# Column sums of a 32768 x 2048 matrix: float16 casting loads and pairwise adds against float32 loads folded in one vector instruction

## The chip, the cores and the metric

The kernel runs on one core of a Trainium2 chip. The core has a tensor engine (PE, matmuls, with PEld for its weight loads), a vector engine (DVE), a scalar engine (ACT), GpSimd (POOL) and a sync engine (SP). SP, ACT and POOL can issue DMA transfers between HBM and the on-chip memory SBUF; the transfers run on 16 DMA engines. Matmul results go to the accumulator memory PSUM. The metric is device time in microseconds. Lower is better.

## The reference

```python
def setup_inputs():
    batch, seq, dim = 32, 1024, 2048
    return {"grad_output": np.random.randn(batch, seq, dim).astype(np.float32)}

def reference(grad_output):
    return np.sum(grad_output, axis=(0, 1)).astype(np.float32)
```

The input is 32768 rows of 2048 float32 numbers, 268.44 MB. The output is one row of 2048 sums.

## The kernel before, in words

The input is seen as a matrix of 32768 rows. A load of m "rows" takes m x 128 matrix rows and gives each of the 128 SBUF partitions m whole matrix rows that lie one behind the other in HBM (`"(p m) d -> p (m d)"`). One row of such a load is 128 x 2048 float32, 1 MiB. The whole input is 256 of them.

A plan, made in Python before anything is issued, lists the loads in order: two float32 loads of one row, issued by SP (PRE_TILES, PRE_ENGS); 30 loads of 8 rows (BULK_M); one of 2; a taper of 4 and 2 (BULK_TAPER); five of one row (TAIL_TILES); and the last row in four column pieces of 512 (COL_SPLIT_LAST). All but the first two are issued by POOL and cast from float32 to float16 on the way (line 146). The 8-row tiles rotate through three buffers (T_BUFS).

For each load of two or more rows DVE adds the first half of the tile to the second half in float16 (line 152), which leaves half as many rows in a tile `c`. PE then multiplies each 512-column piece of `c` by a column of ones (line 161), which sums over the 128 partitions, and accumulates into one of four PSUM banks, one for each quarter of the 2048 columns. One-row tiles go to PE directly. At the end ACT and DVE copy the four banks to SBUF, two each (lines 175 and 177), and SP writes the 8 KB result (line 178).

The order on each engine is that of the program text; a framework inserts the waits. A load into a used buffer waits for the DVE add that read it; an add waits for its load; the matmuls wait for the add.

Of the kernel before, what the change touches and what calls it, by code (L numbers as in the profile page):

```python
# [1 line left out]

# [4 lines left out]

P = 128
MM_N = 512  # L10

PRE_TILES = 2
PRE_M = 1
PRE_ENGS = ("sync", "sync")
BULK_M = 8
BULK_TAPER = (4, 2)
USE_DVE = True
TAIL_TILES = 5
COL_SPLIT_LAST = True
T_BUFS = 3  # L20
C_BUFS = 3
TAIL_BUFS = 8
BULK_ENGS = ("gpsimd",)
OUT_COPY_ENGS = ("scalar", "vector")


@with_exitstack
def kernel(
    ctx: ExitStack,
    tc: tile.TileContext,  # L30
    grad_output: bass.AP,
    out: bass.AP,
):
    nc = tc.nc
    fp32 = mybir.dt.float32
    fp16 = mybir.dt.float16

    D = out.shape[-1]
    flat = grad_output.rearrange("b s d -> (b s) d")
    R = flat.shape[0]  # L40
    assert R % P == 0 and D % MM_N == 0
    nbanks = D // MM_N
    n_row_blocks = R // P

    pre_tiles = min(PRE_TILES, n_row_blocks // PRE_M // 4)
    col_split = COL_SPLIT_LAST and nbanks > 1
    taper = [m for m in BULK_TAPER if m < BULK_M]
    n_small = TAIL_TILES + (1 if col_split else 0)
    while pre_tiles * PRE_M + sum(taper) + n_small > n_row_blocks:
        if TAIL_TILES and n_small > 1:  # L50
            n_small -= 1
        elif taper:
            taper = taper[1:]
        else:
            col_split = False
            n_small = min(n_small, 1)
            break
    n_tail = n_small - (1 if col_split else 0)

    plan: list = []  # L60
    row = 0
    for i in range(pre_tiles):
        plan.append((row, PRE_M, fp32, PRE_ENGS[i % len(PRE_ENGS)], 0, D))
        row += P * PRE_M
    tail_start = R - P * (n_small + sum(taper))
    bi = 0
    while row < tail_start:
        take = min(P * BULK_M, tail_start - row)
        plan.append((row, take // P, fp16, BULK_ENGS[bi % len(BULK_ENGS)], 0, D))
        bi += 1  # L70
        row += take
    for m in taper:
        plan.append((row, m, fp16, BULK_ENGS[bi % len(BULK_ENGS)], 0, D))
        bi += 1
        row += P * m
    for _ in range(n_tail):
        plan.append((row, 1, fp16, BULK_ENGS[bi % len(BULK_ENGS)], 0, D))
        bi += 1
        row += P
    if col_split:  # L80
        for b in range(nbanks - 1, -1, -1):
            plan.append((row, 1, fp16, BULK_ENGS[bi % len(BULK_ENGS)], b * MM_N, MM_N))
            bi += 1
        row += P
    assert row == R

    io_pool = ctx.enter_context(tc.tile_pool(name="io", bufs=T_BUFS))
    pre_pool = None
    if pre_tiles:
        pre_pool = ctx.enter_context(tc.tile_pool(name="pre", bufs=pre_tiles))  # L90
    c_pool = None
    if USE_DVE:
        c_pool = ctx.enter_context(tc.tile_pool(name="csum", bufs=C_BUFS))
    n_small_tiles = n_tail + (nbanks if col_split else 0)
    tail_pool = None
    if n_small_tiles:
        tail_pool = ctx.enter_context(
            tc.tile_pool(name="tail", bufs=min(n_small_tiles, TAIL_BUFS))
        )
    const_pool = ctx.enter_context(tc.tile_pool(name="const", bufs=1))  # L100
    psum_pool = ctx.enter_context(tc.tile_pool(name="psum", bufs=1, space=bass.MemoryType.PSUM))

    ones16 = const_pool.tile([P, 1], fp16)
    nc.vector.memset(ones16[:], 1.0)  # L104
    ones32 = None
    if pre_tiles:
        ones32 = const_pool.tile([P, 1], fp32)
        nc.vector.memset(ones32[:], 1.0)  # L108

    accs = [  # L110
        psum_pool.tile([1, MM_N], fp32, tag=f"psum{b}", name=f"psum{b}")
        for b in range(nbanks)
    ]
    res = const_pool.tile([1, D], fp32)

    def uses_dve(entry) -> bool:
        _, m, dt_, _, _, col_n = entry
        return USE_DVE and dt_ is fp16 and m > 1 and col_n == D

    def n_chunks(entry) -> int:  # L120
        _, m, dt_, _, _, col_n = entry
        n = (m * col_n) // MM_N
        return n // 2 if uses_dve(entry) else n

    total_mm = [0] * nbanks
    for e in plan:
        for j in range(n_chunks(e)):
            total_mm[((e[4] + j * MM_N) % D) // MM_N] += 1
    started = [False] * nbanks
    n_mm = [0] * nbanks  # L130

    for i, entry in enumerate(plan):
        row0, m, dt_, eng_name, col_lo, col_n = entry
        rows = flat[row0 : row0 + m * P]
        if col_n == D:
            src = rows.rearrange("(p m) d -> p (m d)", p=P)
        else:
            src = rows[:, col_lo : col_lo + col_n]

        if dt_ is fp16:  # L140
            big = m > 1 and col_n == D
            pool, tag = (io_pool, "T") if big else (tail_pool, "Ttail")
            T = pool.tile([P, m * col_n], fp16, tag=tag, name=f"t{i}")
        else:
            T = pre_pool.tile([P, m * col_n], fp32, tag="Tpre", name=f"t{i}")
        getattr(nc, eng_name).dma_start(out=T[:], in_=src)  # L146

        red = T
        if uses_dve(entry):
            half = (m * col_n) // 2  # L150
            C = c_pool.tile([P, half], fp16, tag="C", name=f"c{i}")
            nc.vector.tensor_tensor(  # L152
                out=C[:], in0=T[:, :half], in1=T[:, half:], op=mybir.AluOpType.add
            )
            red = C

        w = ones16 if dt_ is fp16 else ones32
        for j in range(n_chunks(entry)):
            b = ((col_lo + j * MM_N) % D) // MM_N
            n_mm[b] += 1  # L160
            nc.tensor.matmul(  # L161
                accs[b][:, :],
                lhsT=w[:],
                rhs=red[:, j * MM_N : (j + 1) * MM_N],
                start=(not started[b]),
                stop=(n_mm[b] == total_mm[b]),
            )
            started[b] = True

    bank_order = list(range(nbanks - 1, -1, -1)) if col_split else list(range(nbanks))  # L170
    for k, b in enumerate(bank_order):
        eng = OUT_COPY_ENGS[k % len(OUT_COPY_ENGS)]
        dst = res[:, b * MM_N : (b + 1) * MM_N]
        if eng == "scalar":
            nc.scalar.copy(out=dst, in_=accs[b][:, :])  # L175
        else:
            nc.vector.tensor_copy(out=dst, in_=accs[b][:, :])  # L177
    nc.sync.dma_start(out=out[None, :], in_=res[:])


# [1 line left out]
_INS = ['grad_output']  # L182
_OUTS = [((2048,), 'float32')]


# [23 lines left out]
```

## Time and profile before

| | |
|---|---|
| timed runs | 628.96 us median of 3 (628.45 to 629.14) |
| profiled execution | span 627.2 us from the first to the last instruction; the profile holds no other time of this execution |
| PE | busy 195.1 us (31%), 536 matmuls, mean granted clock 0.65 of full |
| DVE | busy 138.9 us (22%), 37 instructions |
| POOL | busy 22.6 us (4%), 42 of its instructions issue loads |
| DMA | queue of the casting loads: 6048 packets, 133.17 MB written, 98.9% of the 16 engines' span |
| HBM | 268.44 MB read, 428 GB/s over the span |

A row of instructions names the line in the kernel, the engine, the operation, what it writes and reads (out<-in) with sizes, how often, the busy time and the mean duration in ns, and then the idle time of the engine ahead of it with what ended that idle time. The page's DMA row gives the busy share of the DMA engines in 40 equal slices of the span, as one digit each in tenths (9 is 90% or more). Bytes in the DMA queues are those written, so a casting load counts half of what it reads.

### The profile page before, as it was taken

To read this page: it belongs to the slowest core of one execution; us is meant where nothing else is said; L and a number is where in the kernel's file an instruction comes from. 1 tells how busy PE (TensorE), PEld (TensorE's weight loads), DVE (VectorE), ACT (ScalarE), POOL (GpSimd) and SP (SyncE) were. 2 spreads that over 40 slices of the span, in tenths; PEclk is the share of its full clock that TensorE was granted. 3 is DMA by queue.
4 is the path that set the end of the run, shared out by engine and by line. 5 is a ranking of instruction groups with operands and counts; after the bars stand their busy time and mean duration, and the time that the engine had idled before them with its cause. 6 is when DMAs were issued, how large, how long until landed. Compare 5 with 4: busy or idle time off the path is not lost.

```text
span 627.2 us, 1267 instructions
## 1 busy us (share of the span) xinstructions
PE 195.1 (31%) x536; PEld 58.1 (9%) x536; DVE 138.9 (22%) x37; ACT 2.4 (0%) x3; POOL 22.6 (4%) x46
## 2 busy tenths in 40 slices
PE   3323320333203333123341134321333312343165
PEld 0001100011000111001110011100111000111011
DVE  0202222022220122211222202222022221122320
ACT  0000000000000000000000000000000000000000
POOL 1000000000000000000000000000000000000110
PEclk9677556775567665667655776656676567665677
DMA  9999999999999999999999999999999999999997
GB/s 242 226 234 201 234 201 234 202 232 203 232 203 232 203 232 203 232 204 230 205 230 205 230 205 230 205 230 206 228 207 228 207 224 211 224 211 221 206 206 139
DMA packets 6344, 135.36 MB, mean 216 GB/s; under 512 B 705, under 2 KB 1217, under 8 KB 1857
## 3 DMA queue, kind: packets, MB, share of 16 engines
q0 software_dynamic: 6048, 133.17, 98.9%
q1 hardware_dynamic: 290, 2.11, 0.9%
q8 instruction: 4, 0.07, 0.0%
q14 instruction: 2, 0.02, 0.0%
HBM read 268.44 MB, written 0.01 MB: 428 GB/s over the span
## 4 chain that ended last, share of the span: by engine, by line
another core or an unknown queue 66%; DVE 21%; DMA 11%; PE 1%; POOL 1%; issue 0%; DVEq 0%; POOLq 0%
DVE c L152 20%; DMA t<-in_grad_output_dram 11%; PE psum L161 1%; POOL t L146 1%; DVEq L152 0%; DVE res L177 0%; POOLq L193 0%
## 5 line engine op out<-in xcount | busy, mean ns | idle before, releaser
L161 PE MATMUL psum<-c,ones 128*1 128x512 f16 x496 | 175.9, 533 | 405.5 <-DVE c L152 405.5
L152 DVE TENSOR_TENSOR c<-t 128x8192 f16<-128x8192 f16 (+2 forms) x33 | 137.5, 4167 | 471.1 <-DMA t<-in_grad_output_dram 471.1
L161 PEld LDWEIGHTS <-ones 128*1 128x1 f16 x520 | 56.5, 109 | 537.5 <-issue 516.4
L146 POOL DMA_DIRECT2D t<-in_grad_output_dram x42 | 22.4, 538 | 590.4 <-DVE c L152 575.3
L161 PE MATMUL psum<-t,ones 128*1 128x512 f16 (+1 forms) x40 | 19.4, 639 | 23.5 <-DMA t<-in_grad_output_dram 23.5
L177 DVE COPY res<-psum 1x512 f32<-1x512 f32 x2 | 1.4, 679 | 13.9 <-PE psum L161 13.9
L161 PEld LDWEIGHTS psum<-t,ones 128*1 128x1 f32 x16 | 1.6, 106 | 27.5 <-DMA t<-in_grad_output_dram 14.1
L175 ACT COPY res<-psum 1x512 f32<-1x512 f32 x2 | 1.1, 575 | 621.1 <-PE psum L161 621.1
L175 ACT ACT_TABLE_LOAD x1 | 1.3, 1283 | 0.7 <-PEq L193 0.7
L104 DVE MEMSET ones<- 128x1 f16 x1 | 0.1, 59 | 0.8 <-PEq L193 0.8
L193 POOL MEMSET const-float32-0.0<- 128x1 f32 x1 | 0.1, 100 | 0.2 <-issue 0.2
L193 POOL MEMSET const-bfloat16-1.0<- 128x1 bf16 x1 | 0.1, 103 | 0.0
L193 POOL MEMSET const-float32-1.0<- 128x1 f32 x1 | 0.1, 100 | 0.0
L193 POOL MEMSET const-uint8-127<- 128x1 uint8 x1 | 0.1, 100 | 0.0
L108 DVE MEMSET ones<- 128x1 f32 x1 | 0.1, 59 | 0.0
## 6 DMA issues: line engine op xcount, KB each, us to landing
t<-in_grad_output_dram POOLq DMA_DIRECT2D x30, 4096.0 KB, 53.1
t<-in_grad_output_dram POOLq DMA_DIRECT2D x5, 512.0 KB, 20.4
t<-in_grad_output_dram SPq DMA_DIRECT2D x2, 1024.0 KB, 14.3
t<-in_grad_output_dram POOLq DMA_DIRECT2D x2, 1024.0 KB, 26.6
t<-in_grad_output_dram POOLq DMA_DIRECT2D x1, 2048.0 KB, 29.0
t<-in_grad_output_dram POOLq DMA_DIRECT2D x4, 128.0 KB, 16.1
out_dram<-res SPq DMA_DIRECT2D x1, 8.0 KB
```

The source lines that it names most:

```text
L104: nc.vector.memset(ones16[:], 1.0)
L108: nc.vector.memset(ones32[:], 1.0)
L146: getattr(nc, eng_name).dma_start(out=T[:], in_=src)
L152: nc.vector.tensor_tensor(out=C[:], in0=T[:, :half], in1=T[:, half:], op=mybir.AluOpType.add)
L161: nc.tensor.matmul(accs[b][:, :], lhsT=w[:], rhs=red[:, j * MM_N : (j + 1) * MM_N], start=(not started[b]), stop=(n_mm[b] == total_mm[b]),)
L175: nc.scalar.copy(out=dst, in_=accs[b][:, :])
L177: nc.vector.tensor_copy(out=dst, in_=accs[b][:, :])
L193: nc = _bacc.Bacc("TRN2", target_bir_lowering=False, num_devices=1)
```

## The change

The kernel body is written anew. All loads are float32 and issued by SP. UNITS lists them: 7, 8 and 7 rows ten times over, then 7, 7, 6, 4, 3, 2, 2, 2, 2 (39 units, 255 rows); the last row comes in two pieces, three quarters of the columns and one quarter. The units rotate through three slots of one SBUF tile `ring`; a slot has room for its 7 or 8 rows and one more row in front. For i of 3 and up, SP waits until unit i-3 has been summed by PE (`s_free`) before it issues unit i.

For a unit of m > 2 rows, DVE folds the rows 1 to m-1 into the row in front with one `tensor_reduce`, whose view of the rows runs over m innermost, so that consecutive elements read lie 2048 elements apart. For a unit of 2 rows DVE only passes a semaphore on. PE then sums the folded row and the unit's row 0 (or the two rows of a 2-row unit) over the partitions: 8 float32 matmuls of 512 columns, in which quarter g of the columns goes to column group 32 x g of the array and to PSUM partition 32 x g. The three first quarters share one bank, the last has its own. These matmuls stand in a hardware loop of 13 rounds over the three slots. After the sums of slots 0 and 1, PE also runs six float16 matmuls of a zero tile into a spare bank (FILL).

At the end DVE copies the three first quarters and SP writes them; ACT copies the last quarter and writes it itself; POOL waits for both. The PSUM banks are set to zero by DVE at the start, as no matmul starts an accumulation. The code stands in a `tile_critical` block, in which the waits are written by hand; the program has an additional rendezvous of the engines with POOL where the block begins and one where it ends.

The core of the diff, with the planning code, the pools and the final launch code left out:

```diff
-BULK_M = 8
-BULK_TAPER = (4, 2)
-TAIL_TILES = 5
-BULK_ENGS = ("gpsimd",)
+SLOTS = (7, 8, 7)
+UNITS = SLOTS * 10 + (7, 7, 6, 4, 3, 2, 2, 2, 2)
+FILL = (6, 6, 0)
...
-            T = pool.tile([P, m * col_n], fp16, tag=tag, name=f"t{i}")
-        getattr(nc, eng_name).dma_start(out=T[:], in_=src)
-            nc.vector.tensor_tensor(
-                out=C[:], in0=T[:, :half], in1=T[:, half:], op=mybir.AluOpType.add
-            )
-        for j in range(n_chunks(entry)):
-            b = ((col_lo + j * MM_N) % D) // MM_N
-            nc.tensor.matmul(
-                accs[b][:, :],
-                lhsT=w[:],
-                rhs=red[:, j * MM_N : (j + 1) * MM_N],
...
+    def sums(at, c0=0, w=D):
+        for g in range(4):
+            lo, hi = max(c0, g * Q), min(c0 + w, (g + 1) * Q)
+            if lo < hi:
+                mm = t.matmul(
+                    (acc if g < 3 else accr)[32 * g : 32 * g + 1, lo - g * Q : hi - g * Q],
+                    lhsT=ones[:],
+                    rhs=ring[:, at + lo - c0 : at + hi - c0],
+                    start=False,
+                    stop=False,
+                    tile_position=(0, 32 * g),
+                    skip_group_check=True,
+                )
+        return mm
...
+        for i, m in enumerate(UNITS):
+            s = i % len(SLOTS)
+            at = base[s] + (D if m > 2 else 0)
+            src = flat[row * P : (row + m) * P].rearrange("(p m) d -> p (m d)", p=P)
+            if i >= len(SLOTS):
+                q.wait_ge(s_free, i - len(SLOTS) + 1)
+            q.dma_start(out=ring[:, at : at + m * D], in_=src).then_inc(landed[s], 16)
+            row += m
+        at = base[-1] + 2 * D
+        for c0, w, s in ((0, 3 * Q, last[0]), (3 * Q, Q, last[1])):
+            q.dma_start(
+                out=ring[:, at + c0 : at + c0 + w], in_=flat[row * P :, c0 : c0 + w]
+            ).then_inc(s, 16)
...
+        for i, m in enumerate(UNITS):
+            s = i % len(SLOTS)
+            r1 = base[s] + 2 * D
+            v.wait_ge(landed[s], 16 * (i // len(SLOTS) + 1))
+            if m > 2:
+                v.tensor_reduce(
+                    out=ring[:, base[s] : base[s] + D],
+                    in_=ring[:, r1 : r1 + (m - 1) * D].rearrange("p (m d) -> p d m", m=m - 1),
+                    op=add,
+                    axis=X,
+                ).then_inc(red[s], 1)
+            else:
+                v.sem_inc(red[s], 1)
+        t.wait_ge(s_one, 4)
+        with t.Fori(0, len(UNITS) // len(SLOTS)) as _:
+            for s in range(len(SLOTS)):
+                t.wait_ge(red[s], 1)
+                t.sem_inc(red[s], -1)
+                sums(base[s])
+                sums(base[s] + D).then_inc(s_free, 1)
+                for _ in range(FILL[s]):
+                    t.matmul(
+                        junk[0:1, :],
+                        lhsT=fill[:, :1],
+                        rhs=fill[:],
+                        start=True,
+                        stop=True,
+                        tile_position=(0, 0),
+                    )
+        t.wait_ge(last[0], 16)
+        sums(at, 0, 3 * Q).then_inc(s_end[0], 1)
+        t.wait_ge(last[1], 16)
+        sums(at + 3 * Q, 3 * Q, Q).then_inc(s_end[1], 1)
+        v.wait_ge(s_end[0], 1)
+        v.tensor_copy(out=res[0:96, :], in_=acc[0:96, :]).then_inc(s_res[0], 1)
+        a.wait_ge(s_end[1], 1)
+        a.copy(out=res[96:97, :], in_=accr[96:97, :]).then_inc(s_res[1], 1)
...
+        a.dma_start(out=out[None, 3 * Q :], in_=res[96:97, :]).then_inc(s_out[1], 16)
+        for s in s_out:
+            nc.gpsimd.wait_ge(s, 16)
```

## The prediction

> **What bounds the kernel now.** I read the page first (span, DMA row, queues), then the waits, the chain, the timeline at both ends, and last the rows that can price the new instructions.
>
> ```profile
> span 627.2 us, 1267 instructions
> DMA  9999999999999999999999999999999999999997
> q0 software_dynamic: 6048, 133.17, 98.9%
> q1 hardware_dynamic: 290, 2.11, 0.9%
> HBM read 268.44 MB, written 0.01 MB: 428 GB/s over the span
> ```
>
> The 16 DMA engines are full from the first slice to the last. The cast halves what is written (135 MB), not what is read: 268.44 MB, and those bytes stay. On q0, 42 loads x 128 partitions are 5,376 packets and 42 x 16 the rest: each partition's contiguous rows travel as one packet, 64 KB read in an 8-row load.
>
> The waits say that compute stands behind the loads (total, times, longest):
>
> ```profile
> DVE c L152 <- DMA t<-in_grad_output_dram: 471.1, 33, 26.5
> POOL t L146 <- DVE c L152: 575.3, 30, 29.2
> ```
>
> In the chain, start then duration, "unknown queue" is the wait for the next load:
>
> ```profile
> 66.06 4.43 DVE c L152
> 70.49 14.89 another core or an unknown queue
> ...
> 109.23 15.75 another core or an unknown queue
> ```
>
> The head and the tail, in the timeline:
>
> ```profile
> 0.74 0.87 SPq L146 DMA_DIRECT2D t<-in_grad_output_dram  x2
> 5.74 6.11 PE L161 MATMUL psum<-t,ones 128*1 128x512 f32 x8 [5.74 <-DMA t<-in_grad_output_dram]
> 25.86 0.13 PEld L161 LDWEIGHTS psum<-t,ones 128*1 128x1 f32 x1 [0.72 <-issue]
> 26.71 0.13 PEld L161 LDWEIGHTS psum<-t,ones 128*1 128x1 f32 x1 [0.72 <-issue]
> 27.41 4.42 DVE L152 TENSOR_TENSOR c<-t 128x8192 f16<-128x8192 f16 x1 [26.51 <-DMA t<-in_grad_output_dram]
> 28.59 0.08 PEld L161 LDWEIGHTS psum<-t,ones 128*1 128x1 f32 x1 [0.34 <-issue]
> 29.02 0.08 PEld L161 LDWEIGHTS psum<-t,ones 128*1 128x1 f32 x1 [0.34 <-issue]
> 46.74 4.43 DVE L152 TENSOR_TENSOR c<-t 128x8192 f16<-128x8192 f16 x1 [14.90 <-DMA t<-in_grad_output_dram]
> ...
> 620.52 3.57 PE L161 MATMUL psum<-t,ones 128*1 128x512 f16 x8 [0.96 <-DMA t<-in_grad_output_dram]
> 624.13 0.68 DVE L177 COPY res<-psum 1x512 f32<-1x512 f32 x1 [0.17 <-PE psum L161]
> 624.90 0.32 SPq L178 DMA_DIRECT2D out_dram<-res  x1
> ```
>
> 27.41, 46.74, 66.06: 8 MiB every 19.32 us, 434.2 GB/s. So the kernel is one stream of reads, plus 2 to 3 us before it and some 4.5 us behind it. The change can win only in the stream's rate, its two ends, or the one interval that was 0.97 us too long (15.75 against 14.78). It can lose wherever it breaks the stream.
>
> **The change, part by part.** Unit means one load of UNITS.
>
> *Loads (from POOL, cast, to SP, uncast).* Leaving: 42 POOL issues of 0.54 us. Arriving: 41 SP issues of about 0.4 us (two took 0.87), 17 us that lie beside transfers. The price to find is the rate of a float32 load. The two small float32 loads on SP in the head show it, 8 KB per packet; below, the window's bounds, then busy times, then granted clock, DMA share, GB/s written:
>
> ```profile
> 3.00:5.50 2.50, 0.00 (x0) 0.00 (x0) 0.00 (x0) 0.00 (x0) 0.00 (x0) 1.00 1.00 423
> ```
>
> Writing all four bytes did not halve the rate: 423 GB/s at 8 KB, against 434.2 read at 64 KB. As time per packet and engine that is 8192 x 16 / 423 GB/s = 309.9 ns, and 19.32 us / 8 = 2,415 ns. The line through both is 9.2 ns per packet plus 0.0367 ns per byte. The new loads put 41 x 8 = 328 packets on each engine, mostly of 56 KB: 16.78 MB x 0.0367 + 328 x 9.2 ns = 615.9 + 3.0 = **618.9 us**. Ends: 615.9 (no packet cost) and 268.44 MB / 423 GB/s = 634.6. I take 618.9, because 56 KB is nearest to the 64 KB row.
>
> *Head.* The first 1 MiB was consumed 5.00 us after its issue (0.74 to 5.74); 8 x 309.9 ns of that is stream, so 2.52 is fixed. The changed program has one more rendezvous of all engines with POOL ahead of the loads: 0.2 us, from 0 to the 0.74 that all setup took. The last bytes are then usable at 0.74 + 0.2 + 2.52 + 618.9 = **622.4**. Same sum on the kernel before: 0.74 + 2.52 + 2 x 2.48 + 8 x 2.415 = 27.54, where the first big load was consumed at 27.41.
>
> *Fold on DVE.* 33 float16 adds (137.5 us) go; 35 float32 folds come, reading 212 rows x 2048 = 434,176 elements. No row reads with a step, which the fold does (consecutive elements lie 8 KB apart). Nearest rows:
>
> ```profile
> L152 DVE TENSOR_TENSOR c<-t 128x8192 f16<-128x8192 f16 x30 | 132.8, 4425 | 459.7 <-DMA t<-in_grad_output_dram 459.7
> L152 DVE TENSOR_TENSOR c<-t 128x4096 f16<-128x4096 f16 x1 | 2.3, 2293 | 8.5 <-DMA t<-in_grad_output_dram 8.5
> L177 DVE COPY res<-psum 1x512 f32<-1x512 f32 x2 | 1.4, 679 | 13.9 <-PE psum L161 13.9
> ```
>
> The adds give 0.52 ns per output and 0.16 us fixed; the float32 copy fits twice that, 512 x 1.04 + 146 = 679. Per element read the ends are 0.27 (4425/16384) and 1.33 ns (679/512); I take 1.04, the float32 step. A 7-row unit folds 6 rows: 12,288 x 1.04 + 160 = 12.9 us; an 8-row unit 15.1. Their loads take 16.9 and 19.3, so the fold hides, even at 1.33 (16.3 and 19.1). Total 457 us, 73% of the span. Two PSUM memsets of 512 columns, new on DVE, lie ahead of the first landing at 20.4 (0.74 + 0.2 + 2.52 + 16.9). The cover is gone at 16.9/12,288 = 1.38 ns.
>
> [...]
>
> *Slots.* A slot is free 12.9 + at most 6.8 (matmuls) = 20 us after landing; its next transfer starts two loads later, at 34, less 2.5 of latency. SP's queue, which holds every later load behind that wait, has 11 us to spare. Behind those waits stand only SP's output and, through POOL, the end.
>
> *PE.* 536 matmuls become 39 x 8 + 4 float32 ones, plus 156 idle float16 ones that write to a spare bank. The timeline's weight loads stand 0.43 us apart at the high clock and 0.85 at the low one: that is a float32 matmul. Eight one by one are 3.4 to 6.8 us, well under 16.9, so the middle hides them. At the end 2-row units land every 4.83 us; I take it that the four column groups run together (0.9 to 1.8 us per unit), so nothing is queued when the last bytes land. Bounds: together, 0; one by one, 5.4 (third rival).
> [...]
>
> *Tail.* The kernel before queues eight matmuls at the low clock (3.57 us), copies, and ends 2.4 us after the last copy's end at 624.81. Now: one matmul 0.43 (0.85 if slow) + 0.15, the ACT copy 0.58 + 0.04, the same 2.4 from there to the end, with the output now issued by ACT itself, and 0.2 for the added rendezvous: 3.8 to 4.2. The DVE copy and SP's output of the other three quarters start 0.6 us of stream earlier and hide.
>
> **Sum.** 622.4 + 3.8 to 4.2 = 626.2 to 626.6, so 626.4, against the profiled span of 627.2. The three timed runs have a median of 628.96, 1.8 us above that span; I carry the 1.8: **628.2 us**, 0.1% down. Measurement can tell about 0.2% (1.26 us) from no change, so this counts as no change. My own spread on it is 627.0 to 629.4.
>
> **The rivals.**
> - *Packets cost nothing, or part of the 9.2 ns.* Speaks for it: the casting stream moves 64 KB in 2,415 ns, 0.4% over the line's slope. Against: the 423 window. 615.9 + 3.5 + 3.8 + 1.8 = **625.0**, up to 627 with part of the cost.
> - *Rows are cut to 8 KB packets on SP's queue.* For it: the only SP packets seen are 8 KB. Against: their rows were no longer, and POOL's queue sends 64 KB whole. 634.6 in place of 618.9: **643.9**. It is slower than before as soon as the stream takes over 620.9 (432 GB/s).
> - *Column groups run one by one.* For it: the matmuls in the timeline do, but all in one column group, which is what speaks against. Fold of the 3-row unit ends 16.8 us before the last landing; then 3.4 + 1.3, 3.4, 3.4 + 1.3, 3.4 + 1.3, 3.4, 1.3, 0.43 us of PE work end 5.85 after it instead of 0.43: **633.6**. Decides once a 2-row unit with its idle matmuls approaches 4.83 us.
> - *DVE becomes the bound, the other side's clearest case.* For it: nothing shows that a read with a step takes one step of 1.04 ns. Against: no row, contiguous or from PSUM, is above 1.33. Two steps per element, 2.08 ns: 434,176 x 2.08 = 903 us + 35 x 0.16, behind a first landing at 20.4, ahead of units 37 and 38 and the last row (2.5 + 4.8 + 4.8 + 2.4) and the tail (4), plus 1.8: **950**. From 1.38 ns on it decides.
>
> **How the numbers follow.** Forecast 58% (same 42, faster 13, slower 3); cheap packets 20% (faster 19, same 1); one by one 10%; small packets 6%; DVE 6%, these three all slower. Faster 0.32, same 0.43, slower 0.25. The range from 624.8 to 633.8 leaves out the small packets and DVE, and a little below.
>
> **What would show it.** Right: landings 16.9 and 19.3 us apart, the fold rows near 12.9 and 15.1 us, DVE waiting for DMA with 4 us in each load, DMA share full throughout, the last matmul less than 1 us after the last landing. Wrong: fold rows above 17 us; SP's queue waiting for PE shortly before a gap in the DMA row; packets in the thousands more than 41 x 144; matmuls still queued from 2-row units after the last landing; landings over 17.1 us apart for 7 rows. A difference between span and timed runs other than 1.8 us would shift everything alike.

## The result

The changed kernel takes **777.78 us** (median of four runs, 777.56 to 778.92), the kernel before 628.99 (628.45 to 629.14). The ratio is 1.237 (95% interval 1.2353 to 1.2388): 23.7% slower, where 628.2 us was forecast.

The page of the profile after, the lines that answer to those of before, with DVE's row of busy tenths added:

```profile
span 777.1 us, 1791 instructions
DVE  0999999999999999999999999999999999999970
DMA  9999976999698698779869769986986987786456
q1 hardware_dynamic: 5910, 268.44, 82.6%
HBM read 268.44 MB, written 0.01 MB: 345 GB/s over the span
```

DVE's row is what DMA's was before: full from the first landing to nearly the end. The DMA engines now have holes, so the loads are no longer the bound.

The groups of the profile after on DVE, one row per shape (count, total us, mean ns, then the idle time ahead):

```profile
L98 DVE TENSOR_REDUCE ring<-ring 128x2048 f32<-128x12288 f32 x22 | 460.3, 20965 | 17.9 <-DMA ring<-in_grad_output_dram 17.9
L98 DVE TENSOR_REDUCE ring<-ring 128x2048 f32<-128x14336 f32 x10 | 243.9, 24393 | 0.0
L98 DVE TENSOR_REDUCE ring<-ring 128x2048 f32<-128x10240 f32 x1 | 17.6, 17558 | 0.0
L98 DVE TENSOR_REDUCE ring<-ring 128x2048 f32<-128x6144 f32 x1 | 7.2, 7183 | 0.0
L98 DVE TENSOR_REDUCE ring<-ring 128x2048 f32<-128x4096 f32 x1 | 4.5, 4474 | 0.0
```

A fold of 6 rows takes 20.97 us and one of 7 rows 24.39; their loads bring the next rows in 16.9 and 19.3. Per element that is 1.71 and 1.70 ns, over the 1.38 at which the cover is gone. The small folds of 2 and 3 rows stay near the price taken, 1.09 and 1.17 ns.

The waits of the profile after (total, times, longest), first of the engines, then of SP's queue:

```profile
PE acc L60 <- PEq L112: 597.0, 37, 41.4
DVE ring L98 <- DMA ring<-in_grad_output_dram: 17.9, 1, 17.9
```

```profile
SPq L80 <- PE accr L60: 744.4, 36, 42.8
```

DVE waits for a load once, for the first. From there the chain runs backward: PE waits for the fold (L112 is its wait), SP's queue waits for PE to free the slot, and the loads wait in that queue. The timeline of DVE at the start, and of the last folds and loads:

```profile
20.38 111.24 DVE L98 TENSOR_REDUCE ring<-ring 128x2048 f32<-128x12288 f32 x5 [17.89 <-DMA ring<-in_grad_output_dram]
```

```profile
722.94 29.05 DVE L98 TENSOR_REDUCE ring<-ring 128x2048 f32<-128x10240 f32 x3
...
743.99 15.01 SPq L80 DMA_DIRECT2D ring<-in_grad_output_dram  x4
...
759.04 1.05 SPq L84 DMA_DIRECT2D ring<-in_grad_output_dram  x2
```

The span is 20.4 us to the first landing, 731.6 of folds without a gap, and 25.1 from the last fold's end (752.0) to the end: the last 2-row loads and the last row, which were issued late because slots came free late.

### The profile page after: what moved, and what is told of

Read it like the earlier page. It is cut to its first block, busy times and chain, and to the rows that moved or that the text cites. A ratio compares the mean times of both kernels' runs of the same rounds, so it can differ in the third digit from the quotient of the medians.

```text
span 777.1 us, 1791 instructions
## 1 busy us (share of the span) xinstructions
PE 176.6 (23%) x788; PEld 33.6 (4%) x788; DVE 733.6 (94%) x40; ACT 1.9 (0%) x2; POOL 0.2 (0%) x4
## 3 DMA queue, kind: packets, MB, share of 16 engines
q1 hardware_dynamic: 5910, 268.44, 82.6%
## 5 line engine op out<-in xcount | busy, mean ns | idle before, releaser
L98 DVE TENSOR_REDUCE ring<-ring 128x2048 f32<-128x12288 f32 (+4 forms) x35 | 731.6, 20982 | 17.9 <-DMA ring<-in_grad_output_dram 17.9
L60 PE MATMUL acc<-ring,ones 128*1 128x512 f32 x474 | 132.0, 976 | 597.0 <-PEq L112 597.0
L60 PE MATMUL accr<-ring,ones 128*1 128x512 f32 x158 | 130.7, 977 | 0.0
L116 PE MATMUL junk<-fill 128*1 128x512 f16 x156 | 50.9, 476 | 0.0
L60 PEld LDWEIGHTS acc<-ring,ones 128*1 128x1 f32 x474 | 16.0, 101 | 682.2 <-issue 681.1
L116 PEld LDWEIGHTS junk<-fill 128*1 128x1 f16 x156 | 16.8, 108 | 56.4 <-issue 49.9
L60 PEld LDWEIGHTS accr<-ring,ones 128*1 128x1 f32 x158 | 12.9, 101 | 0.5 <-DMA ring<-in_grad_output_dram 0.5
## 6 DMA issues: line engine op xcount, KB each, us to landing
ring<-in_grad_output_dram SPq DMA_DIRECT2D x1, 256.0 KB, 12.9
```

The lines of the kernel that those rows point to most:

```text
L60: mm = t.matmul((acc if g < 3 else accr)[32 * g : 32 * g + 1, lo - g * Q : hi - g * Q], lhsT=ones[:], rhs=ring[:, at + lo - c0 : at + hi - ...
L98: v.tensor_reduce(out=ring[:, base[s] : base[s] + D], in_=ring[:, r1 : r1 + (m - 1) * D].rearrange("p (m d) -> p d m", m=m - 1), op=add, a ...
L116: t.matmul(junk[0:1, :], lhsT=fill[:, :1], rhs=fill[:], start=True, stop=True, tile_position=(0, 0),)
```

## The experiments

After the result the open question was why an element costs 1.7 ns. Four theories were set against each other: A, reading one element from each row in turn has its own price; B, the 8 KB distance between the rows collides with something of that size; C, the loads that write SBUF at the same time slow DVE; D, a reduction is slow as such.

### Folds alone: number of rows, distance, order, loads

The kernel holds only folds, of rows loaded once, first with other loads running and later again, from the fold of 6 rows on without; its output is one of the fold results, not the sums.

```diff
+    def rows(n, pitch, w):
+        return big[:, : n * pitch].rearrange("p (m d) -> p d m", m=n)[:, :w, :]
...
+    red(rows(2, D, D), D)   # and 3 to 8 rows
+    red(big[:, : 6 * D].rearrange("p (d m) -> p d m", m=6), D)   # 6 neighbours per output
+    red(big[:, : 6 * 512].rearrange("p (b m d) -> p b d m", m=6, d=2), 512)   # step 2, 4, 8, 16, 64, 256
+    red(rows(6, 512, 512), 512)   # distances 512 to 3072
```

> One unit is loaded, then DVE runs folds of several forms, first with no transfer running, then with float32 loads running beside it. Nothing of the reference's sum is computed; each fold's own duration is what is wanted. In the changed kernel folds of 2, 3, 5, 6, 7 rows took 4.47, 7.18, 17.56, 20.97, 24.39 us, 1.09, 1.17, 1.71, 1.71, 1.70 ns per element. Theory A (rows in rotation): the price is set by the number of rows that are read in turn, loads or no loads: about 1.05 ns at 2 rows and 1.7 from 5 rows in both phases, at any pitch; a contiguous fold of 6 near 1.04 ns (12.9 us). Theory B (the 8 KB pitch): with the row pitch moved off 2048 elements by a few elements the price falls from 1.7 to near 1.04 ns. Theory C (the loads' writes take the memory): in the first phase all folds cost near 1.04 ns (6 rows 12.9 us) and in the second 1.7 ns (21 us), except where no load happens to run. Theory D (the instruction itself is slow): the contiguous fold of 6 also takes 21 us.

The groups of this kernel (L34 is the helper that records each fold; x2 is the same fold in the first part and again in the second, where from 6 rows on no load runs beside it; the row of 12288 holds two folds of rows and two of neighbours):

```profile
L34 DVE TENSOR_REDUCE o<-big 128x2048 f32<-128x12288 f32 x4 | 67.6, 16899 | 0.1
L34 DVE TENSOR_REDUCE o<-big 128x2048 f32<-128x16384 f32 x2 | 55.3, 27671 | 0.1
L34 DVE TENSOR_REDUCE o<-big 128x2048 f32<-128x14336 f32 x2 | 48.5, 24258 | 0.1
L34 DVE TENSOR_REDUCE o<-big 128x2048 f32<-128x10240 f32 x2 | 34.9, 17432 | 0.1
L34 DVE TENSOR_REDUCE o<-big 128x2048 f32<-128x8192 f32 x2 | 28.0, 14018 | 0.1
L34 DVE TENSOR_REDUCE o<-big 128x2048 f32<-128x6144 f32 x2 | 14.4, 7192 | 0.1
L34 DVE TENSOR_REDUCE o<-big 128x2048 f32<-128x4096 f32 x2 | 8.9, 4463 | 27.1 <-DMA big<-in_grad_output_dram 27.0
```

The single instructions of the trace, in ns:

```
rows of 2048, one element of each in turn    2: 4462   3: 7191   4: 14019   5: 17432   6: 20846   7: 24258   8: 27670
the same, second time                        2: 4464   3: 7192   4: 14017   5: 17432   6: 20846   7: 24259   8: 27672
6 neighbours per output, 2048 outputs        12952 and 12952
512 outputs of 6, step in elements           2: 3353   4: 5595   8: 5592   16: 5272   64: 5325   256: 5326
512 outputs of 6, distance 512 to 3072       5324 to 5326 (2048: 5324);  2049: 5469  2050: 5750  2052: 5610  2056: 5581;  2064 to 2560: 5324 or 5325
```

- **D falls.** The same instruction over neighbours takes 12,952 ns, 12,288 x 1.04 + 0.16 us to within 1%.
- **C falls.** The loads had ended before 320 us (0 GB/s from 320 us on, where windows around the first folds show 447 and 456); the folds of 6, 7 and 8 rows behind that point differ from the first ones by at most 2 ns. The loads ran in the first part and not, as was meant, in the second, but either order separates the two.
- **B falls.** Distances of 2 KB to 12 KB cost the same. Moving the rows 1 to 8 elements off the 8 KB makes it 3 to 8% dearer, not cheaper, and from 16 elements on it costs 5,324 ns again.
- **A stands, with a shape that no theory had.** From 4 rows on each further row costs 3,413 ns, 1.667 ns per element, 1.6 times the 1.04. Up to 3 rows nearly the speed of neighbours holds (1.09 and 1.17 ns per element against 1.05). So it does for a step of 2 elements (8 bytes, 3,353 ns for 3,072 elements, 1.09 each); a step of 4 (16 bytes, 5,595 ns) already pays what 8 KB pays (5,324).

Two or three rows in rotation run nearly as fast as neighbours do, although each element lies 8 KB from the one before it, while six in rotation are slow from a step of 16 bytes on. No run shows by what mechanism.

### The fold left out

```diff
-            if m > 2:
+            if False:
...
-                sums(base[s])
+                sums(base[s] + D)
```

> The fold is left out (DVE only passes the semaphore on; PE sums a unit's first row twice), so the rows 1 to m-1 are missing from the result. Loads, slots, matmuls and the end stay. If the fold alone made the kernel slow: back to the time of the loads, 628 us by the prediction's sum (stream 618.9 us), between 625 and 630. If the float32 loads themselves are slower (423 GB/s as in the small loads): about 644. If the chain of three slots or the matmuls hold the loads up: above 650.

Measured: 629.81 us (629.69 to 629.96), ratio 1.0015 (1.0005 to 1.0024). The page:

```profile
span 627.9 us, 1791 instructions
DMA  9999999999999999999999999999999999999996
HBM read 268.44 MB, written 0.01 MB: 428 GB/s over the span
```

Landings stand 16.94 and 19.35 us apart. In its timeline PE's sums show when a load is usable: the first, and the last row's two pieces.

```profile
20.57 1.02 PE L60 MATMUL acc<-ring,ones 128*1 128x512 f32 x3 [20.57 <-PEq L112]
...
622.75 1.03 PE L60 MATMUL acc<-ring,ones 128*1 128x512 f32 x6
...
623.35 1.02 PE L60 MATMUL accr<-ring,ones 128*1 128x512 f32 x2
```

The stream is as forecast to 0.8 us (20.57 to 623.35 = 602.8; 20.4 to 622.4 = 602.0 was forecast), and what follows the last landing takes 4.55 us where 3.8 to 4.2 was forecast. So the fold holds 148 of the 149 us between the two kernels.

### The same fold, the same elements, in the order in which they lie

The most direct test: same instruction, same bytes, one view turned round (the result is then not the column sums).

```diff
-                    in_=ring[:, r1 : r1 + (m - 1) * D].rearrange("p (m d) -> p d m", m=m - 1),
+                    in_=ring[:, r1 : r1 + (m - 1) * D].rearrange("p (d m) -> p d m", m=m - 1),
```

> The changed kernel with one word of the fold's view moved: tensor_reduce reads the same 6 or 7 rows of float32 in the order in which they lie, six or seven neighbours per output, and not one element from each row in turn. The same instructions, elements, loads, waits and matmuls; the result is not the column sums. Theory (the order of reading sets the price, all else in the change is hidden): folds of 6 rows take 12.95 us and of 7 rows 15.1, DVE waits for DMA before nearly every fold, landings stand 16.9 and 19.3 us apart, and the time is 629.8 to 630.3, that of the kernels without the fold or with adds. Rival (something else in the change, the slots, the hardware loop or PE's clock while it waits for DVE, holds part of the 150 us): the time stays over 640.

Measured: 631.72 us (631.16 to 632.25), ratio 1.0045 (1.0029 to 1.0062). 146 of the 149 us are gone with one word of a view. Its groups on DVE:

```profile
L98 DVE TENSOR_REDUCE ring<-ring 128x2048 f32<-128x12288 f32 x22 | 285.0, 12952 | 80.3 <-DMA ring<-in_grad_output_dram 80.3
L98 DVE TENSOR_REDUCE ring<-ring 128x2048 f32<-128x14336 f32 x10 | 150.9, 15086 | 64.0 <-DMA ring<-in_grad_output_dram 64.0
L98 DVE TENSOR_REDUCE ring<-ring 128x2048 f32<-128x10240 f32 x1 | 10.8, 10820 | 1.6 <-DMA ring<-in_grad_output_dram 1.6
L98 DVE TENSOR_REDUCE ring<-ring 128x2048 f32<-128x6144 f32 x1 | 6.5, 6542 | 0.0
L98 DVE TENSOR_REDUCE ring<-ring 128x2048 f32<-128x4096 f32 x1 | 4.4, 4409 | 0.0
```

These are the 12.9 and 15.1 us of the prediction, with 80.3 / 22 = 3.7 us of wait ahead of a 6-row fold. Yet it is 1.4 to 1.9 us over what was expected. The stretches of 5 us near the end say where, first this kernel, then the one without the fold (after the window: busy time of PE, PEld, DVE, ACT, POOL, then PE's clock, DMA share, GB/s):

```profile
600.00:605.00 5.00, 3.38 (x17) 0.57 (x18) 5.00 (x2) 0.00 (x0) 0.00 (x0) 0.50 0.97 380
605.00:610.00 5.00, 5.00 (x35) 1.52 (x34) 0.80 (x1) 0.00 (x0) 0.00 (x0) 0.82 0.87 301
```

```profile
600.00:605.00 5.00, 3.17 (x22) 0.84 (x22) 0.00 (x0) 0.00 (x0) 0.00 (x0) 1.00 0.99 419
605.00:610.00 5.00, 1.90 (x16) 0.34 (x16) 0.00 (x0) 0.00 (x0) 0.00 (x0) 1.00 0.99 423
```

(380 + 301 - 419 - 423) x 5 us is 0.8 MB less in 10 us, 1.9 us at 423 GB/s. There the folds of 5, 3 and 2 rows stand one behind the other (idle 0.0 in the groups for the last two), the slots come free late, and the last 2-row loads are issued late: the two loads of the last row leave SP at 612.54 against 608.62. PE has a part in it: in the first stretch its clock is 0.50 against 1.00, and in the second it is busy throughout with the sums and idle matmuls that had queued. No run separates the two parts. The slot arithmetic of the prediction was made for the 7- and 8-row units alone.

### Full sums by other instructions: adds, smaller folds, PE alone

Three kernels that compute all sums with the loads of the changed kernel. In the first DVE halves the rows with contiguous float32 adds:

```diff
-                v.tensor_reduce(
...
+                fold(ring, base[s], r1, m - 1).then_inc(red[s], 1)
...
+            ins = v.tensor_tensor(
+                out=ring[:, o : o + h * D],
+                in0=ring[:, lo : lo + h * D],
+                in1=ring[:, lo + (n - h) * D : lo + n * D],
+                op=add,
+            )
```

> The same fold made of contiguous float32 adds instead of the one strided instruction: the last half of the rows is added to the first half until one row is left (6 rows: adds of 3, 1 and 1 rows). By 1.04 ns per output and 0.16 us each: 10.67 + 0.5 = 11.2 us per 7-row unit and 12.8 + 0.6 = 13.4 per 8-row unit, under their loads of 16.9 and 19.3. If the strided read is the cause: 628 us, like the kernel without the fold, DVE waiting for loads. If DVE is slowed by the loads' writes to SBUF (1.7 ns per output): 17.9 and 21.4 us, DVE stays the bound, about 680 us. If DVE is not what the time hangs on: 778.

630.32 us (630.2 to 630.63), ratio 1.0024 (1.0014 to 1.0034): 0.5 us above the kernel without the fold, and 2.3 above the expected 628, which had taken over the forecast's stream and tail. In its groups 102 adds take 393.8 us where 35 folds took 731.6, and DVE waits for the loads again:

```profile
L83 DVE TENSOR_TENSOR ring<-ring 128x2048 f32<-128x2048 f32 (+2 forms) x102 | 393.8, 3861 | 207.8 <-DMA ring<-in_grad_output_dram 205.4
```

In the second each fold takes at most 3 rows in turn, and PE sums the two or three results:

```diff
+        sizes = [3] * (n // 3) + ([2] if n % 3 == 2 else [])
...
+                    ins = v.tensor_reduce(
+                        out=ring[:, dst : dst + D],
+                        in_=ring[:, r1 + r * D : r1 + (r + n) * D].rearrange("p (m d) -> p d m", m=n),
```

> The changed kernel with the same strided instruction, but over at most three rows at a time: 6 rows are folded as 3 + 3, 7 rows as 3 + 3 with the seventh left to PE, and PE sums three or four rows per unit in place of two; the result is the full sum. The probe's fold of 3 rows took 7.19 us, so a 7- or 8-row unit takes 14.4 us on DVE against a load of 16.9 or 19.3. If the number of rows read in turn sets the price: DVE waits for loads again and the time is that of the adds, 630 to 631 us. If any strided fold costs 1.67 ns per element inside the full kernel: 20.6 us per unit, DVE the bound, about 720 us.

634.41 us (633.69 to 634.98), ratio 1.0086 (1.0071 to 1.0101). The price of 3 rows in turn holds in the full kernel:

```profile
L114 DVE TENSOR_REDUCE ring<-ring 128x2048 f32<-128x6144 f32 x68 | 483.5, 7113 | 122.5 <-DMA ring<-in_grad_output_dram 121.4
```

So reading with a step is not dear as such: 14.4 us for 6 rows hides, 20.97 does not. The 4 us over the expectation arise where those of the turned-round view arose: DVE works on the tapering units until 608.5 us, the loads behind them start late, and the page has 327 GB/s in the last slice but one of the span, where the kernel without the fold has 431. Over a slice of 15.8 us that is 1.6 MB, some 4 us of stream.

In the third DVE does nothing and PE sums every row, first written out, then in a hardware loop:

```diff
-                sums(base[s])
-                sums(base[s] + D).then_inc(s_free, 1)
+            for k in range(m):
+                mm = sums(at0 + k * D)
+            mm.then_inc(s_free, 1)
```

> PE sums every row of a unit, DVE folds nothing; the result is the full sum. In the changed kernel a row's four matmuls (two passes each, four column groups side by side) took 1.7 us at the low clock and 0.85 at the high one, so 7 rows are 6 to 12 us against a load of 16.9. If the loads set the time: 626 to 629, the same as the kernel without the fold. If PE is slowed by reading more or the column groups run one after another (3.4 us a row): 24 us per unit, about 870.

632.76 us (632.63 to 633.04), ratio 1.0062 (1.0045 to 1.0079). That is 3 us above the kernel without the fold and over the expected 626 to 629. PE is busy 47%, so it is not the bound. Its page has a queue that the changed kernel's has not:

```profile
q8 instruction: 16, 0.26, 0.2%
```

16 pieces of 16 KB of instructions are fetched while the loads stream, each one packet of 0.9 to 1.1 us; the program that grew is PE's. With 30 units in a loop:

```diff
+        with t.Fori(0, 10) as _:
+            for s in range(len(SLOTS)):
+                unit(s, SLOTS[s])
```

> PE sums every row as in the unrolled variant, which took 632.8 us with 16 instruction loads of 16 KB on the DMA engines, but the first 30 units stand in a hardware loop of 10 rounds; the result is the full sum. If the instruction loads cost the 3 us: 629.5 to 630.3 us, as without the fold, and few or no instruction loads. If PE's own work at the end costs it (rows summed late, low clock): 632 to 633 us.

631.04 us (630.89 to 631.58), ratio 1.0035 (1.0023 to 1.0047):

```profile
q8 instruction: 3, 0.05, 0.0%
```

13 fetches fewer, 1.7 us less, but not the expected 629.5 to 630.3. The landings in the traces say where the rest lies. Each load ends in 16 landings, and what needs the load waits for the last of them. In the load that follows PE's first fetch (at 45.2 us) of the unrolled kernel, one landing of the 16 falls back: the last comes 1.56 us behind the first, where in the load before it was 0.58. It stays behind in every later load. In the last load of all, the last landing is behind the first by

```
us, last row's second piece   first to last landing   profiled span
without the fold              0.57                    627.9
PE alone, in a loop           2.33                    629.6
PE alone, written out         3.60                    630.9
```

So the fetches are the whole distance: 1.8 us for three of them and 3.0 for 16, as in the spans. None of these kernels is faster than the kernel before: with the fold priced right, the float32 stream itself brings nothing.

### The kernel before with less work behind the stream

The kernel before has such fetches too, four of them (at 113.86, 268.48, 425.43 and 577.58 us, packets of 0.89 to 0.98 us), and one interval of its stream was 0.97 us too long. The next five kernels are made from it. First, deeper float16 adds, so that PE has four matmuls per load and fewer instructions:

```diff
+            n = m
+            while n > 1:
+                n //= 2
+                half = n * col_n
...
+                    out=C[:], in0=red[:, :half], in1=red[:, half : 2 * half], op=mybir.AluOpType.add
```

> The kernel before, with DVE adding each casting load down to one row (halves added three times in float16 for 8 rows) so that PE runs 4 matmuls per load in place of 16; the full sum. Its PE program shrinks from about 1050 to 320 instructions. In the profile before one interval between loads was 0.97 us too long, in the stretch where the first of four instruction loads ran. If these loads of PE's instructions cost that time: 627.8 to 628.3 us. If it was something else: 628.96 like before. DVE's 8 us per load stays under 19.3.

628.75 us (628.2 to 629.1), ratio 0.9995 (0.9986 to 1.0004): no difference. One fetch was left, and the interval around it was long (19.98 us against 19.32), like that around the first of the four in the kernel before. The other three of the four lengthened none (19.40, 19.35 and 19.37 us between the landings around them). The landings of the kernel before show why; of the 16 of each load, this many come more than 0.9 us behind the first:

```
load complete at (us)        104.69   124.98   260.19   279.59   434.18   603.29
fetches since the start           0        1        1        2        3        4
late landings of 16               0        1        1        2        3        4
last behind first (us)         0.33     1.28     1.21     1.28     1.28     1.26
```

After each fetch one more landing is late, by about the same time, and stays late to the end. As the load waits for its last landing, the first late one sets the price, and the further ones, late by as much, add nothing here. That each fetch held up another one of the 16 DMA engines is a guess of mine that is not shown: the records do not name the engine. Second, with the last column piece cut to 128 columns in a bank of its own:

```diff
+    widths = [128, 384] + [MM_N] * (D // MM_N - 1)
```

> The one before it (three levels of float16 adds), and besides the last row's last column piece is 128 columns wide in a PSUM bank of its own (512, 512, 512, 384, 128); the full sum. After the last landing a matmul of 128 columns and a copy of 128 remain, 0.1 to 0.2 and 0.3 us in place of 0.43 and 0.68, and PE has less queued. Expected 0.4 to 1.0 us below the one before it: 626.9 to 627.9 us. If small packets or the extra waits eat it: the same as that one.

628.41 us (627.55 to 628.92), ratio 0.999 (0.9981 to 0.9999): 0.3 us below the one before it, less than expected and within the spread of the runs. The fetch fell at 290.4 us. The chain of this kernel (start, duration, what), three intervals:

```profile
267.60 11.22 another core or an unknown queue
278.84 4.44 DVE c L159
286.92 12.11 another core or an unknown queue
299.05 4.44 DVE c L159
307.13 11.22 another core or an unknown queue
```

12.11 in place of 11.22: the wait for the load during which the fetch ran is 0.89 us longer, about the time that the fetch's packet took (0.94). Third, three loads' one-row sums added together before PE:

```diff
+                if held is not None:
+                    S = c_pool.tile([P, D], fp16, tag="S", name=f"s{i}")
+                    nc.vector.tensor_tensor(out=S[:], in0=held[:], in1=red[:], op=mybir.AluOpType.add)
...
+                if n_held < GROUP:
+                    continue
```

> The kernel of the run best, in which DVE also adds the one-row sums of three 8-row loads together in float16 before PE reads them; PE has about 200 instructions left instead of about 280. Theory (an instruction load of PE takes a DMA engine for some 0.9 us and lengthens the interval around it): no instruction load is left, every interval of the 8-row loads is 19.3 us, and the time is about 0.9 us below best, 627.4 to 627.7. Rival (the long interval has another cause, for instance the place in HBM or a refresh): one interval of about 20.2 us stays, and the time stays at 628.4. DVE has about 1.1 us more per 8-row load and stays far below 19.3.

628.6 us (627.98 to 629.15), ratio 0.9993 (0.9984 to 1.0002). A miss, and a telling one: the fetch was not gone but moved to 613.8 us. The long interval is gone (the last 8-row load is consumed at 588.13, in the second kernel at 588.92), and the last one-row load is consumed at 620.53, hardly earlier (620.66 in the second): the 0.8 us came back where the fetch now lay. Fourth, idle matmuls in the last one-row tiles:

```diff
+        if dt_ is fp16 and m == 1 and col_n == D and i >= len(plan) - nbanks - FILL_TILES:
+            for _ in range(FILL):
+                nc.tensor.matmul(junk[:, :], lhsT=ones16[:], rhs=red[:, :MM_N], start=True, stop=True)
```

> best2_groups with four idle float16 matmuls into a spare bank after each of the last four one-row tiles. Theory (PE's low clock at the end costs what the queued float16 matmuls of the last one-row tiles take beyond the last landing): the granted clock at the end rises, the last matmul ends closer to the last landing, and the time falls by another 0.5 to 0.75 us, to 626.7 to 627.2. Rival (the idle matmuls themselves delay the last sums, or the clock does not rise in time): no gain, or up to 1 us more, 627.4 to 628.5.

628.14 us (627.79 to 628.56), ratio 0.9989 (0.998 to 0.9997). The last slice's clock is 0.9 in place of 0.6, and SP issues the output at 624.12 in place of 624.67; the gain is the 0.5 us of the expectation, the level of 626.7 to 627.2 is not reached: the fetch is still there, at 613.5 us. Last, ten loads' sums together:

```diff
-GROUP = 3
+GROUP = 10
```

> best3_warm with ten 8-row loads' one-row sums added together on DVE, and not three: PE has 35 matmuls fewer. In best2_groups and best3_warm one instruction load of 16 KB is left, at 613.8 and 613.5 us, in the stream's last part, where best had it at 290.4. Theory (an instruction load costs the stream some 0.8 us wherever it falls): the load is gone, the last matmuls start 0.8 us earlier, and the time is 627.2 to 627.5. Rival (it cost nothing there, the end is set by the buffers of the last one-row loads): the load is gone and the time stays at 628.0 to 628.3.

**627.62 us** (627.36 to 628.46), ratio to the kernel before 0.9981 (0.9972 to 0.999). That is 0.1 us over the expected range. No fetch on q8 is left in the page (two of 8 KB, 0.32 us each, remain on a second instruction queue, q14), and its timeline ends so:

```profile
619.84 1.03 PE L183 MATMUL psum<-t,ones 128*1 128x128 f16 x5 [0.57 <-DMA t<-in_grad_output_dram]
...
621.57 1.16 PE L183 MATMUL psum<-t,ones 128*1 128x512 f16 x5
621.98 1.21 ACT L200 COPY res<-psum 1x512 f32<-1x512 f32 x3 [619.96 <-PE psum L183]
622.20 1.14 DVE L202 COPY res<-psum 1x512 f32<-1x512 f32 x2 [13.37 <-PE psum L183]
623.43 0.32 SPq L203 DMA_DIRECT2D out_dram<-res  x1
```

The last one-row load is consumed 0.68 us earlier than with the fetch (620.52), and the output leaves 0.69 earlier. Of the 1.5 us that the output's issue gained on the kernel before (624.90 to 623.43), 0.69 came with the fetch, 0.55 with the idle matmuls (clock 0.9 in the last slice), and 0.23 with the steps before. By its median it is the fastest kernel of the case, 0.19% below the kernel before.

## Why the prediction was wrong

- **The step that failed** is the fold's price: "Per element read the ends are 0.27 and 1.33 ns; I take 1.04, the float32 step." Rows read in turn cost 1.71 ns (20,965 / 12,288). 1.04 is right for neighbours (12,952 ns), so the working was right for an access that the change does not make. The bounds were taken from rows that all read neighbours; they bounded another operation. The text said that no row reads with a step and still closed the upper end at 1.33, below the 1.38 that mattered. (For the 8-row units the cover is gone sooner, at 19.3 us / 14,336 = 1.35 ns.)
- **The rival "DVE becomes the bound"**, given 6%, was right in kind, with its sign and its point of decision, 1.38 ns. Its price of two steps, 2.08 ns, no run shows; 6 and 7 rows in turn cost 1.71 and 1.70 ns, 1.6 times the step taken, and 2 and 3 rows 1.09 and 1.17. With the measured folds its own sum is 20.4 + 731.6 + 18.5 + 1.8 = 772; the rest is the end, 25.1 us in place of 18.5, since the last loads had not been issued in time.
- **The stream** (618.9, packets of whole 56 and 64 KB, 5,910 on q1) and the head were right: 0.17 us late at the first landing, 0.95 at the last. The rivals of cheap packets and of 8 KB packets fall with that.
- **The slots** were right for 7 and 8 rows, wrong for the taper: 1.9 us in the kernel with the view turned round, where DVE and PE both fell behind. So even at 1.04 ns per element the time would have been 631.7 and not 628.2, slower than before.
- **PE**: the forecast took the four column groups to run together without a row that showed it; they do run side by side, so the rival of one by one falls. But one float32 matmul is two records (39 x 8 + 4 = 316 matmuls are 632 records on line 60: 474 and 158), and the 0.43 us taken for a matmul is half of one; the 536 matmuls counted in the kernel before hold 8 float32 ones twice. A 2-row unit at the high clock (1.00 granted from 600 us to the end of the kernel without the fold) takes four steps of 0.43, 1.7 us and not 0.9; at 4.9 us between landings that costs nothing. Side by side, four groups pass in one step of 0.43 us, which is what a single record took in the timeline of the kernel before (weight loads at 28.59 and 29.02, clock 1.00), so the speed-up is 4. The timeline of the kernel without the fold shows two steps, one row:

```profile
621.42 0.60 PE L60 MATMUL acc<-ring,ones 128*1 128x512 f32 x3
621.44 0.59 PE L60 MATMUL accr<-ring,ones 128*1 128x512 f32 x1
621.85 0.61 PE L60 MATMUL acc<-ring,ones 128*1 128x512 f32 x3
621.87 0.59 PE L60 MATMUL accr<-ring,ones 128*1 128x512 f32 x1
```

- **The tail** took 4.55 us in the kernel without the fold, 0.35 over the upper end of 3.8 to 4.2. At the high clock, which was granted there (1.00), the sum was 3.8: the last matmul, with its two records, took 1.06 us up to the copy and not 0.58, and the end came 2.9 us after ACT's copy and not 2.6; the 1.8 us between span and timed run held (1.9 without the fold).

## What to carry to other kernels

A bound taken from rows of another access pattern is no bound: where an operand is read in an order that no row shows, leave the upper end open, and ask how far the price may rise before the cover is gone. Here a rise of a third was enough, and 1.6 times came. If rows must be folded on DVE, add them contiguously or fold three at a time (630.3 and 634.4 us here); and in a kernel that is one full stream of reads, do the slot arithmetic for the tapering loads at the end too, since that is where a slower consumer first reached the end here (1.9 us with the view turned round, some 4 us with the folds of three rows).

## What the runs showed of the hardware that was not expected

- A float32 reduction that takes one element from each of n rows of 2048 in turn ran, in the kernel of folds alone, at 1.09 and 1.17 ns per element for n = 2 and 3 and at 1.69 to 1.71 for n = 4 to 8 (14,019 ns for 4 rows against 7,191 for 3). For 6 rows the distance (2 to 12 KB: 5,324 to 5,326 ns for 3,072 elements) made no difference but for offsets of 1 to 8 elements from 8 KB (5,469 to 5,750), and for 6 to 8 rows neither did concurrent loads (437 and 433 GB/s in the windows from 27 to 100 and 100 to 200 us, which hold the first of them, and 0 beside the second; at most 2 ns in 27,670).
- For 512 outputs of 6 the break in the step lay between 8 bytes (3,353 ns for 3,072 elements) and 16 bytes (5,595).
- In the kernel before, whose stream fills all 16 engines (98.9% on its queue), the first fetch of 16 KB of instructions, a packet of 0.98 us, made one interval 0.97 us too long, for good: from then on one of the 16 landings of every load came 1.20 to 1.30 us behind the first. The second, third and fourth fetch each made one more landing late by as much and cost nothing further. One fetch was worth 0.66 us in the kernel with the deeper adds, 0.89 in the one after it and 0.68 in the last; in the kernel with PE alone written out, 16 of them cost 3.0 us.
